# Hybrid layer with a two-level expert stage on one core: smaller expert blocks, longer weight runs, gathers that skip empty slots, another order of products and outputs

## The chip, the cores and the metric

One core of a Trainium2 chip runs the whole layer as one program. The metric is device time in microseconds, the median of several runs. A core has a matrix engine (TensorE, PE in the profile, with PEld for its weight loads), VectorE (DVE), ScalarE (ACT), GpSimd (POOL) and SyncE (SP), which mostly issues transfers, and 16 DMA engines.

## What is computed

A layer over 512 latent tokens (and 256 context tokens) of width 1024. After the mixer (convolution and gated linear attention, one output projection, a layer norm), each token is routed to one of four groups and to two experts in it:

```python
group_prob = softmax(tok @ wgr + bgr);  p_g, g_idx = top_k(group_prob, 1)
sel = expert_logits[group g_idx];       top_w, top_i = top_k(softmax(sel), 2)
for e in range(16):                     # D_MODEL 1024, D_EXPERT 512
    act = silu(tok @ w1[e]) * (tok @ w3[e])
    out = out + combine[:, e:e + 1] * (act @ w2[e])
x = layer_norm(alpha * x + g2 * out)
```

`tok` is the normed mixer output, scaled and shifted by a condition (`modulate`). All weights are f32: 2 MB each for `w1[e]`, `w3[e]` and `w2[e]`, 96 MB for the 16 experts.

## The kernel before

The first half (to about 316 us) is the mixer: projections in f32 split into two parts (`hi` and `lo`, three products for one), the scans, the output projection, the norm. The normed tokens go to DRAM as `tokd` (L940), the residual part to `yd`.

The expert stage works on slots. After routing, the experts are ranked by their token counts; rank j has `CAPS[j]` slots (L45) and the ranks run in the order `ORDER` (L46). Two first jobs (`NE`, `NE + 1`) take up to 128 tokens of experts 0 and 1 before the ranks are known. What is over a capacity is redone by the loop at the end (L1583), which here has no passes.

- A job with 128 or 256 slots is a `BigJob` (L1216) of one or two blocks of 128. Its weights are split by `split` (L377): ScalarE casts a piece to `whi` (L389), VectorE, for some pieces POOL, subtracts to `wlo` (L391). `load` transposes the gathered rows to `Xh`/`Xl` (hi and lo, L1204 to L1206). `hidden` makes per half `c` of the 512 hidden columns the products with `w1` and `w3` (256 columns each, eight steps of contraction, three products a step), then silu and the gate (L1252, L1253) and a transpose. `outputs` makes 24 products of 512 columns, multiplies into `ob` (L1269) and scatters with an add into `yd` (L1182).
- A job with 64 or 32 slots is a `SmallJob` (L1280): `R` = 2 or 4 column groups side by side in one PSUM tile, plain f32 weights without a split, `ob` at L1340. The last job (`obw`, L1336) skips the scatter; its share is added by a product in `finish`.
- Each expert's weights come as six pieces of 1 MB (L978 to L999): `w1` and `w3` cut by columns (`[128, 8, 256]`, runs of 1 KB in DRAM), `w2` by rows (`[128, 2, 1024]`, runs of 4 KB). The pieces go through a ring of twelve buffers (`RING`, L986), issued on SP's queue in job order. 12 of the 96 pieces are issued before 356 us.
- `gather` (L1175) is an indirect DMA from `tokd` on POOL's queue. Empty slots read the 128 zero rows behind the tokens (L890, L896); their indices are T and up (`dumc`, L1025).
- The main loop (L1481) does for job n: issue the weights of job n + 1, `hidden` of n, one-hot tables for later jobs, `load` of n + 1, `prep_next` (slot indices and gather of n + 3), `outputs` of n. The tile framework may reorder instructions within an engine by need and priority; buffers have fixed counts (`whi` and `wlo` four each of half a piece, six PSUM banks for products, two for transposes).
- `finish` (L1513) reads `yd` back, adds the last job, and norms.

Of the kernel before, what the change touches and what calls it, by code (L numbers as in the profile page):

```python
# [62 lines left out]
def layer(ctx: ExitStack, tc: tile.TileContext, a, out, dbg=None):  # L63
# [179 lines left out]
    def ada_fin(pa, parts, bank, prio):  # L243


        s = sb.tile([P, 512], FT, name="adas", tag="as", bufs=2)
        S.copy(s, pa)
        n = len(parts)
        o = bank()[:, :8 * n].rearrange("p (k q i) -> p q k i", i=2, q=n)
        for j in range(4):  # L250
            mm(o[:, :, j, :], s[:, j * P:(j + 1) * P], sel[:, 0:2 * n], prio, start=True, stop=True)
        ts_ = []
        for q, (c0, hf) in enumerate(parts):
            t = sb.tile([P, 4, 2], FT, name="adac", tag="adac", bufs=4)
            V.tensor_tensor(t, o[:, q], vc(VBA + 8 * c0, hf)[:, :, None].to_broadcast([P, 4, 2]), op=OP.add)
            ts_.append(t)
        return ts_

    class Ada:
# [10 lines left out]
        def fin(self):  # L270
            return ada_fin(self.pa, self.parts, pbg, PR_ADA)
# [7 lines left out]
    def ab_half(dst, sh, sc, hf, g0, b0):  # L279

        def bc2(c0):
            return vc(c0, hf)[:, :, None].to_broadcast([P, 4, 2])
# [242 lines left out]
    rb = sb.tile([P, 20], FT, name="rb")  # L525
    V.memset(g4, 0.0)
    with tc.issue_after(wk_lo.ins):
# [6 lines left out]
        G.dma_start(wr[:, :, 4:20], a["router_expert_w"][0].rearrange("(k p) g -> p k g", p=P))  # L534
        G.dma_start(rb[:, 0:4], dview(a["router_group_b"], 0, [[0, P], [1, 4]]))
# [34 lines left out]
    ab2 = const.tile([P, 2, KC, 2], FT)  # L570
# [308 lines left out]
    wsum = sb.tile([P, 2, 20], FT, name="wsum")  # L879
# [10 lines left out]
    tokd = drp.tile([T + P, D], FT, name="tokd")  # L890
# [7 lines left out]
    lg = sb.tile([P, NT, 20], FT, name="lg")  # L898
# [91 lines left out]
    def load_piece(e, ev, n):  # L990
# [4 lines left out]
        shape = [P, 2, 1024] if nm == "expert_w2" else [P, 8, 256]  # L995
# [178 lines left out]

    def gather(idx, R):  # L1175
# [10 lines left out]
    def transpose_to(src, n, dsts):  # L1186

        for j0 in range(0, n, 4):
            pt = pt_()
            m = min(4, n - j0)  # L1190
            transpose4(pt, [src[:, (j0 + j) * P:(j0 + j + 1) * P] for j in range(m)])
            dsts(j0, m, pt)

    def hilo_ev(hi, lo, mod=False):

        def ev(j0, m, pt):
            f = "p k t -> p (k t)"
            for j in range(m if mod else 0):
                A, B = ab2[:, 0, j0 + j, 0:1], ab2[:, 1, j0 + j, 0:1]
# [15 lines left out]

    class BigJob:  # L1216


        def __init__(self, blocks, first=False):
            self.blocks = blocks  # L1220
# [5 lines left out]
        def load(self):  # L1226
            self.X, self.A = [], []
            for _, _, g in self.blocks:
                x = hl_tiles(KC, "X")
                transpose_to(g, KC, hilo_ev(*x, True))  # L1230
                self.X.append(x)

        def hidden(self, wts):
            for b in self.blocks:
                self.A.append(hl_tiles(4, "A"))
            for c in range(2):
                H = []
                for wi in range(2):
                    his, los = split(wts[2 * c + wi], 256, **self.kws(2 * c + wi))
                    for b, (xh, xl) in enumerate(self.X):  # L1240
                        if wi == 0:
                            H.append((pb_(), Bank()))
                        o, grp = H[b]
                        o = o[:, wi * 256:(wi + 1) * 256]
                        for k in range(KC):
                            grp.mm(o, xh[:, k, :], his[k])
                            grp.mm(o, xh[:, k, :], los[k])
                            grp.mm(o, xl[:, k, :], his[k])
                for b, (_, w, _) in enumerate(self.blocks):
                    o = H[b][0]  # L1250
                    s_ = mo.tile([P, 256], FT, name="s", tag="s", bufs=4)
                    S.activation(s_, o[:, :256], AF.Silu)  # L1252
                    V.scalar_tensor_tensor(s_, o[:, 256:], w, s_, op0=OP.mult, op1=OP.mult)  # L1253
                    hi, lo = self.A[b]
                    transpose_to(s_, 2, hilo_ev(hi[:, 2 * c:2 * c + 2], lo[:, 2 * c:2 * c + 2]))

        def outputs(self, wts):
            W = [split(wts[4 + q], 1024, **self.kws(4 + q)) for q in range(2)]
            for (idx, _, _), (ah, al) in zip(self.blocks, self.A):
                os_ = [pb_() for n in range(2)]  # L1260
# [375 lines left out]
```

## Time and profile before

| | |
|---|---|
| median of 3 runs | 704.65 us (703.65 to 704.81) |
| the profiled execution | 701.98 us, of it the span 700.2 us |
| PE busy | 645.3 us (92%) |
| DVE busy | 474.9 us (68%) |
| ACT busy | 318.5 us (45%) |
| POOL busy | 135.2 us (19%) |
| DMA | 176.79 MB, mean 252 GB/s over the span |
| mean granted clock of TensorE | 0.974 |

The span is the time from the first to the last instruction on the core. An engine's busy share is an average over stages; what a stage is worth is read in that stage. A DMA share of about 1 in a stretch means that the 16 DMA engines were busy all through it.

### The profile page before, as it was taken

The numbers are of one execution on the slowest core, as the hardware profiler recorded it, in microseconds if no ns is written. First come the engines' busy times: TensorE is split into PE (matmuls) and PEld (weight loads), VectorE is DVE, ScalarE is ACT, GpSimd is POOL, SyncE is SP. The second block draws the span as 40 slices with busy tenths as digits, with TensorE's granted clock in tenths as the row PEclk, the third lists the DMA queues.
The fourth block names the chain that finished last, engine by engine and source line by source line (L and its number), as shares of the span: only waits on it lengthen the run. The fifth ranks groups of instructions, "written<-read, shape, count | busy, mean of one in ns | idle before, by whom it ended". The sixth has DMA issues, their size and how long they took to land.

```text
span 700.2 us, 11612 instructions
## 1 busy us (share of the span) xinstructions
PE 645.3 (92%) x4378; PEld 505.8 (72%) x4378; DVE 474.9 (68%) x1036; ACT 318.5 (45%) x505; POOL 135.2 (19%) x106
## 2 busy tenths in 40 slices
PE   5899999989999999996798899998999999999973
PEld 4565689777887787784698598594988588996431
DVE  8545741785965877649899875586669887594245
ACT  3338721458432234325276553454557375471100
POOL 2410000000000100025417312032123221122112
PEclk9999999999999999997799999999999999999998
DMA  8997965372112189626469899899999999979943
GB/s 310 370 338 248 313 197 176 121 230 73 59 62 64 57 294 373 204 91 219 165 204 355 314 338 369 263 369 353 359 367 319 324 369 345 348 216 349 318 142 116
DMA packets 114125, 176.79 MB, mean 252 GB/s; under 512 B 3905, under 2 KB 82129, under 8 KB 114066
## 3 DMA queue, kind: packets, MB, share of 16 engines
q1 hardware_dynamic: 107570, 157.31, 65.4%
q0 software_dynamic: 5136, 15.50, 8.9%
q10 hardware_dynamic: 1360, 3.21, 1.2%
q8 instruction: 36, 0.59, 0.3%
q14 instruction: 23, 0.19, 0.1%
HBM read 160.92 MB, written 15.07 MB: 251 GB/s over the span
## 4 chain that ended last, share of the span: by engine, by line
PE 68%; DVE 17%; ACT 6%; DMA 4%; issue 3%; POOL 1%; DVEq 0%; ACTq 0%
PE pb L144 32%; PE mm L144 21%; PE gl L144 3%; PE pt L154 3%; DVE wlo L391 3%; DMA raw<-in_expert_w_dram 3%; ACT whi L389 2%; PE po L144 2%; PE bg L146 2%; PE tp L154 1%; DVE gg L621 1%; PE pt L144 1%; PE py L144 1%; PE pu L144 1%; DVE gg L620 1%
## 5 line engine op out<-in xcount | busy, mean ns | idle before, releaser
L391 DVE TENSOR_TENSOR wlo<-raw,whi 128x1024 fp32r<-128x1024 f32 x65 | 80.3, 1245 | 50.9 <-ACT whi L389 50.4
L144 PE MATMUL pb<-whi,Xh 128*128 128x256 f32 x384 | 110.6, 289 | 3.7 <-ACT Xh L1205 3.7
L144 PE MATMUL pb<-whi,Xl 128*128 128x256 f32 x384 | 110.2, 288 | 1.6 <-DVE Xl L1206 1.6
L144 PE MATMUL pb<-wlo,Xh 128*128 128x256 f32 x384 | 108.9, 285 | 0.0
L389 ACT CAST whi<-raw 128x1024 fp32r<-128x1024 f32 x68 | 70.9, 1049 | 57.6 <-PE mm L144 26.2
L389 ACT CAST whi<-ew 128x1024 fp32r<-128x1024 f32 x68 | 71.3, 1051 | 29.4 <-PE pb L144 28.2
L144 PEld LDWEIGHTS pb<-whi,Xh 128*128 128x128 f32 x384 | 73.3, 191 | 8.0 <-ACT Xh L1205 7.1
L391 DVE TENSOR_TENSOR wlo<-ew,whi 128x1024 fp32r<-128x1024 f32 x56 | 68.8, 1237 | 12.9 <-ACT whi L389 10.9
L144 PEld LDWEIGHTS pb<-whi,Xl 128*128 128x128 f32 x384 | 73.1, 191 | 2.0 <-DVE Xl L1206 2.0
L144 PEld LDWEIGHTS pb<-wlo,Xh 128*128 128x128 f32 x384 | 73.3, 191 | 0.1
L1182 POOL DMA_INDIRECT yd<-ob,idx x18 | 30.6, 1699 | 103.3 <-DVE ob L1340 31.5
L391 POOL TENSOR_TENSOR wlo<-ew,whi 128x1024 fp32r<-128x1024 f32 x12 | 29.9, 2501 | 86.9 <-issue 70.2
L144 PE MATMUL mm<-hhi,whi 128*128 128x512 f32 x112 | 44.3, 403 | 1.6 <-ACT hhi L368 1.6
L144 PE MATMUL mm<-hhi,wlo 128*128 128x512 f32 x112 | 42.8, 392 | 0.0
L144 PE MATMUL mm<-hlo,whi 128*128 128x512 f32 x112 | 42.5, 390 | 0.0
L294 POOL TENSOR_TENSOR ss<-ss,nhalf 128x4 f32<-128x4 f32 x4 | 5.4, 1357 | 188.8 <-DVE ss L293 188.8
L144 PE MATMUL pb<-wlo,Ah 128*128 128x512 f32 x96 | 38.6, 403 | 0.2 <-DVE wlo L391 0.2
L144 PE MATMUL pb<-whi,Ah 128*128 128x512 f32 x96 | 38.8, 404 | 0.0
L144 PE MATMUL pb<-whi,Al 128*128 128x512 f32 x96 | 38.1, 402 | 0.3 <-DVE Al L1206 0.3
L144 PE MATMUL mm<-wlo,hhi 128*128 128x256 f32 x128 | 36.9, 288 | 0.0
L144 PE MATMUL mm<-whi,hhi 128*128 128x256 f32 x128 | 36.7, 287 | 0.0
L144 PE MATMUL mm<-whi,hlo 128*128 128x256 f32 x128 | 36.6, 286 | 0.0
(418 smaller groups left out, 1445.8 us busy)
## 6 DMA issues: line engine op xcount, KB each, us to landing
ew<-in_expert_w_dram SPq DMA_DIRECT2D x64, 1024.0 KB
raw<-in_expert_w_dram SPq DMA_DIRECT2D x32, 1024.0 KB
raw<-in_w_ada_dram SPq DMA_DIRECT2D x22, 1024.0 KB
raw<-in_w_in_dram SPq DMA_DIRECT2D x10, 1024.0 KB
raw<-in_w_out_dram SPq DMA_DIRECT2D x4, 1024.0 KB
xz<-in_x_dram SPq DMA_DIRECT2D x4, 512.0 KB
ada<-in_w_ada_dram SPq DMA_DIRECT2D x2, 1024.0 KB
x<-in_x_dram SPq DMA_DIRECT2D x4, 512.0 KB
```

Of the source, the lines that this page charges most:

```text
L144: return PE.matmul(o, lhsT, rhs, **kw)
L146: return PE.matmul(o, lhsT, rhs, **kw)
L154: PE.transpose(pool_tile[:, j * P:(j + 1) * P], s, ident)
L294: pows.append(G.tensor_tensor(dst, dst, nhalf[:, :dst.shape[1]], op=OP.pow))
L389: S.copy(hi, r[:, k0:k0 + step, :])
L391: lows.append(lo_eng[k0 // step].tensor_tensor(lo, r[:, k0:k0 + step, :], hi.bitcast(FT), op=OP.subtract))
L620: V.tensor_tensor_scan(g[0:DK, :], mask[0:DK, :n], m[0:DK, :], 0.0, op0=OP.mult, op1=OP.add)
L621: V.tensor_tensor_scan(g[DK:P, ::-1], mask[DK:P, :n], m[DK:P, ::-1], 0.0, op0=OP.mult, op1=OP.add)
L1182: G.indirect_dma_start(out=yd.rearrange("t (r w) -> (t r) w", r=R), out_offset=bass.IndirectOffsetOnAxis(ap=idx[:, :1], axis=0), in_=o, in ...
```

## The change

- `CAPS` becomes `[256, 192] + [128] * 5 + [64] * 3 + [32] * 3 + [31] + [0] * 2`, and `ORDER` is new. A job's capacity is cut into blocks of 128, 64 and 32 (`parts_of`); a job of 192 slots is one `Block` of 128 and one `SmallBlock` of 64.
- All pieces are halves by rows, with a partition holding neighbouring rows (`"o (p k) n -> p (o k) n"`): runs of 8 KB for all three weights. The products with `w1` and `w3` now have 512 columns, and a piece holds four of the eight contraction steps for all columns.
- To match, the transposes take every fourth (`rows_of`) or every second (`every`) column of their source, the condition's scale and shift are made a second time in that order (`abx`, from a second set of small products in `ada_fin` and four small loads `pvec`), and the first job's pick products read `x1` in steps of four.
- `gather` has a bounds check, so that empty slots move nothing; the three gather buffers are zeroed once on POOL, and the 128 zero rows of `tokd` and their two stores are gone.
- `hidden` is a generator with a step per piece; `gate` (silu, gate, transposes) follows all products of the job. The first step of the next job is issued ahead of the outputs of this one.

The diff, cut to what the steps below speak of:

```diff
-CAPS = [256] * 3 + [128] * 4 + [64] * 5 + [32, 31] + [0] * 2
-ORDER = [12, 0, 11, 6, 10, 1, 3, 8, 4, 2, 5, 9, 7, 13]
+CAPS = [256, 192] + [128] * 5 + [64] * 3 + [32] * 3 + [31] + [0] * 2
+ORDER = [12, 11, 0, 9, 1, 8, 2, 7, 3, 4, 5, 6, 10, 13]
...
+        for n_, v_ in enumerate((a["b_ada"][0, 3 * D:4 * D], a["b_ada"][0, 4 * D:5 * D], a["ln1_g"][0], a["ln1_b"][0])):
+            G.dma_start(pvec[:, n_], v_.rearrange("(h p c) -> p h c", h=2, c=4))
...
-    sh0, sc0, sh1, sc1 = ada.fin()
+    (sh0, sc0, sh1, sc1), perm = ada.fin(lambda c0, hf: px(c0 - 3, hf))
     ab_half(ab2, sh0, sc0, 0, V1G, V1B)
     ab_half(ab2, sh1, sc1, 1, V1G, V1B)
+    xp = perm()
+    ab_half(abx, xp[0], xp[1], 0, 2, 3, px)
+    ab_half(abx, xp[2], xp[3], 1, 2, 3, px)
...
-        S.dma_start(tokd[T:T + P, h * 512:(h + 1) * 512], zero)
...
-        src = src[:, h * 256:(h + 1) * 256, :] if nm == "expert_w2" else src[:, :, h * 256:(h + 1) * 256]
-        return src.rearrange("o (k p) n -> p (o k) n", p=P)
+        n = src.shape[1] // 2
+        src = src[:, h * n:(h + 1) * n, :]
+        return src.rearrange("o (p k) n -> p (o k) n", p=P)
...
+    gxs = [mo.tile([P, D], FT, name=f"gx{n}") for n in range(3)]
...
     def gather(idx, R):
-        g = mo.tile([P, D // R], FT, name="gx", tag="gx", bufs=3)
+        g = gxs[ngx[0] % 3][:, :D // R]
+        ngx[0] += 1
         ins = G.indirect_dma_start(out=g, out_offset=None, in_=tokd.rearrange("t (r w) -> (t r) w", r=R),
-                             in_offset=bass.IndirectOffsetOnAxis(ap=idx[:, :1], axis=0))
+                             in_offset=bass.IndirectOffsetOnAxis(ap=idx[:, :1], axis=0),
+                             bounds_check=T * R - 1, oob_is_err=False)
...
+    def every(src, c, j):
+
+        return src.rearrange("s (p c) -> s c p", c=c)[:, j]
+
+    def rows_of(g, hf):
+        return [every(g[:, hf * 512:(hf + 1) * 512], 4, c) for c in range(4)]
...
+    class Block:
...
+        def load(self):
+            self.X = hl_tiles(KC, "X")
+            for hf in range(2):
+                pt = pt_()
+                transpose4(pt, rows_of(self.g, hf))
+                hilo_ev(*self.X, True)(4 * hf, 4, pt)
...
+        def products(self, c, wi, his, los):
+
+            xh, xl = self.X
+            for k in range(4):
+                kc = 4 * c + k
+                mm3(self.H[wi], xh[:, kc, :], xl[:, kc, :], his[k], los[k], kc == 0, kc == KC - 1)
...
+    class SmallBlock:
...
+        def load(self):
...
+            if R == 2:
+                transpose4(pt, [every(self.g, 4, c) for c in range(4)])
+                parts = [(slice(0, P), pt.rearrange("p (c r n) -> p c r n", c=4, r=2))]
+            else:
...
+                for u in range(2):
+                    us = slice(u * 64, (u + 1) * 64)
+                    for c in range(4):
+                        mm(pt[us, c * P:(c + 1) * P], every(self.g, 4, c), ident, start=True, stop=True)
...
+    def parts_of(j):
+
+        c, off, parts = cap_of(j), 0, []
+        while off < c:
+            R = next(R for R in (1, 2, 4) if P // R <= c - off or R == 4)
+            parts.append((R, off))
+            off += P // R
+        return parts
...
+    for g in gxs:
+        G.memset(g, 0.0)
     pick(0)
...
+    steps_ = {seq[0]: jobs[seq[0]].hidden(wts[seq[0]])}
     for n_, j in enumerate(seq):
...
-        jobs[j].hidden(wts[j])
+        for _ in steps_[j]:
+            pass
...
         if n_ + 1 < len(seq):
             jobs[seq[n_ + 1]].load()
+        jobs[j].gate()
         prep_next(n_ + 3)
+        if n_ + 1 < len(seq):
+
+            steps_[seq[n_ + 1]] = jobs[seq[n_ + 1]].hidden(wts[seq[n_ + 1]])
+            next(steps_[seq[n_ + 1]])
```

## Rows read from the trace of the kernel before

**Rows 1.** The page, chain that ended last, shares of the span by engine.

```profile
PE 68%; DVE 17%; ACT 6%; DMA 4%; issue 3%; POOL 1%; DVEq 0%; ACTq 0%
```

**Rows 2.** Timeline of DVE (start us, us, line, operation), two result multiplies.

```profile
397.76 0.68 DVE L1269 TENSOR_TENSOR ob<-pb,g2b 128x512 f32<-128x512 f32 x1
...
670.24 1.98 DVE L1336 SCALAR_TENSOR_TENSOR obw<-pb,sa,g2x 31x256 f32<-31x256 f32 x4 [1.61 <-PE pb L144]
```

**Rows 3.** Busy us by stretch: length, PE, PEld, DVE, ACT, POOL, clock, DMA share, GB/s.

```profile
397.80:403.90 6.10, 5.00 (x62) 2.57 (x55) 4.03 (x15) 2.95 (x8) 2.60 (x2) 1.00 0.61 194
403.90:442.60 38.70, 38.70 (x288) 35.09 (x288) 26.39 (x51) 18.51 (x27) 7.73 (x5) 1.00 1.07 351
442.60:454.60 12.00, 11.97 (x80) 5.98 (x77) 3.65 (x11) 4.10 (x10) 1.57 (x1) 1.00 0.82 235
454.60:480.70 26.10, 24.18 (x184) 19.97 (x184) 20.62 (x40) 14.14 (x18) 8.82 (x5) 1.00 1.08 363
480.70:488.60 7.90, 7.87 (x47) 3.37 (x43) 4.10 (x13) 3.44 (x8) 2.54 (x2) 1.00 1.05 381
488.60:528.30 39.70, 39.70 (x295) 37.01 (x295) 27.82 (x52) 21.66 (x33) 8.09 (x5) 1.00 1.07 356
528.30:549.20 20.90, 20.25 (x154) 16.82 (x153) 19.30 (x30) 13.20 (x17) 5.76 (x3) 1.00 1.06 338
549.20:559.40 10.20, 10.17 (x64) 4.79 (x63) 8.39 (x51) 3.72 (x9) 2.88 (x3) 1.00 0.95 286
559.40:583.50 24.10, 21.73 (x149) 18.84 (x149) 22.13 (x34) 17.07 (x24) 5.07 (x3) 1.00 1.07 360
583.50:621.00 37.50, 37.50 (x276) 34.82 (x276) 25.50 (x45) 20.69 (x31) 9.15 (x6) 1.00 0.95 299
621.00:637.00 16.00, 16.00 (x114) 14.12 (x115) 13.36 (x22) 8.69 (x12) 5.25 (x3) 1.00 1.01 313
637.00:649.90 12.90, 12.87 (x95) 6.92 (x95) 2.55 (x6) 1.30 (x4) 1.60 (x2) 1.00 1.06 352
649.90:663.00 13.10, 12.90 (x90) 6.50 (x90) 2.82 (x11) 1.88 (x5) 1.56 (x1) 1.00 1.05 353
663.00:670.20 7.20, 5.92 (x98) 3.00 (x96) 1.20 (x3) 1.88 (x4) 1.55 (x1) 1.00 0.39 61
```

**Rows 4.** PE: a piece of the chain by time, two starts in the timeline, pick products.

```profile
419.69 8.31 PE pb L144 x70
...
366.03 0.39 PE L144 MATMUL pb<-whi,Ah 128*128 128x512 f32 x1
...
368.83 0.40 PE L144 MATMUL pb<-whi,Ah 128*128 128x512 f32 x1
...
339.85 3.84 PE L144 MATMUL pt<-ohf,x 128*128 128x128 f32 x32 [0.26 <-DVE sa L1163]
```

**Rows 5.** Timeline of PE, the outputs of a job of 64 slots.

```profile
659.31 3.65 PE L144 MATMUL pb<-ew,at 128*64 128x512 f32 x14
```

**Rows 6.** The page's row of POOL's DMA queue; SP's issues from 356 us on.

```profile
q0 software_dynamic: 5136, 15.50, 8.9%
...
356.39 10.48 SPq L997 DMA_DIRECT2D ew<-in_expert_w_dram  x6
```

**Rows 7.** Packets in two windows of 4 us, 428 to 432 and 504 to 508.

```profile
DMA packets 1395, 1.40 MB, mean 349 GB/s; under 512 B 30, under 2 KB 1395, under 8 KB 1395
...
DMA packets 481, 1.63 MB, mean 408 GB/s; under 512 B 22, under 2 KB 103, under 8 KB 481
```

**Rows 8.** Timeline of PE, a wait of the first job's products.

```profile
346.92 0.39 PE L144 MATMUL pb<-whi,Xh 128*128 128x256 f32 x1 [1.61 <-ACT Xh L1205]
```

**Rows 9.** Timelines of POOL and DVE while POOL subtracts, and the first gather.

```profile
326.64 7.07 POOL L391 TENSOR_TENSOR wlo<-ew,whi 128x1024 fp32r<-128x1024 f32 x3 [3.41 <-ACT whi L389]
...
341.53 1.10 POOL L1177 DMA_INDIRECT gx<-tokd,idx  x1 [7.82 <-issue]
...
329.05 2.44 DVE L1154 TENSOR_SCALAR ohf<-slot,posr 128x128 f32<-128x128 bf16 x1
```

More of the change, by code (lines that the diff above doesn't have):

```diff
@@ L1324, in outputs @@
+            pt = pt_()
+            transpose4(pt, [every(hs[:, q * 256:(q + 1) * 256], 2, o) for q in range(m // 2) for o in range(2)])
+            v = pt[:, :m * P].rearrange("p (c i g s) -> p i g c s", i=2, g=gw, s=n)
+            for g_ in range(gw):
+                fs = slice(m * g_, m * g_ + m)
+                S.activation(sg[:, fs], v[:, 0, g_], AF.Silu)
+                V.tensor_tensor(self.at[:, fs], v[:, 1, g_], sg[:, fs], op=OP.mult)
         def outputs(self, wts, wide=None):
             R, n = self.R, self.n
[L1326 removed]
@@ L1339, in outputs, with __init__, kws, hidden @@
             ob = mo.tile([P, ow], FT, name="ob", tag="ob", bufs=2)
-            V.scalar_tensor_tensor(ob, po[:, :ow], w, g2x[R], op0=OP.mult, op1=OP.mult)
-            scatter(ob, idx, R)
+            V.scalar_tensor_tensor(ob, po[:, :ow], self.w, g2x[R], op0=OP.mult, op1=OP.mult)
+            scatter(ob, self.idx, R)
+    class BigJob:
+        def __init__(self, blocks, first=False):
+            self.blocks = [Block(*b) for b in blocks if b[-1] == 1]
+            self.small = [SmallBlock(*b) for b in blocks if b[-1] > 1]
+            self.kw, self.pool = dict(prio=0) if first else {}, ()
+        def kws(self, q):
+            return dict(self.kw, lo_eng=(V, G if q in self.pool else V))
+        def load(self):
+            for b in self.blocks + self.small:
+                b.load()
+        def hidden(self, wts):
+            for b in self.blocks + self.small:
+                b.start()
+            for c in range(2):
+                for wi in range(2):
+                    W = split(wts[2 * c + wi], 512, **self.kws(2 * c + wi))
+                    for b in self.blocks:
+                        b.products(c, wi, *W)
+                    if wi:
+                        for b in self.small:
+                            b.products(c, wts)
+                    yield
+        def gate(self):
+            for b in self.blocks + self.small:
+                b.gate()
+        def outputs(self, wts):
+            W = [split(wts[4 + q], 1024, **self.kws(4 + q)) for q in range(2)]
+            for b in self.blocks:
+                b.outputs(W)
+            for b in self.small:
+                b.outputs(wts)
@@ new lines, in layer, with kws, __init__, hidden @@
+    class FirstJob(BigJob):
+        def kws(self, q):
+            if q < 2:
+                return dict(prio=0, after=lsc, lo_eng=(G, G), lo_after=pows[-1])
+            return BigJob.kws(self, q)
+    class SmallJob:
+        def __init__(self, blocks):
+            self.blocks = [SmallBlock(*b) for b in blocks]
+        def load(self):
+            for b in self.blocks:
+                b.load()
+        def hidden(self, wts):
+            for b in self.blocks:
+                b.start()
+            for c in range(2):
+                for b in self.blocks:
+                    b.products(c, wts)
+                yield
+        def gate(self):
+            for b in self.blocks:
+                b.gate()
+        def outputs(self, wts, wide=None):
+            for b in self.blocks:
+                b.outputs(wts, wide)
@@ L1461, in last_hot @@
         jl = seq[-1]
-        R = jobs[jl].R
+        R, = [R for R, _ in parts_of(jl)]
         n, w = P // R, D // R
@@ L1604, in layer @@
             load_piece(-1, fev, q)
-        job = BigJob([(idx, w, gather(idx, 1)[0])])
+        job = BigJob([(idx, w, gather(idx, 1)[0], 1)])
         job.load()
-        job.hidden(wts[-1])
+        for _ in job.hidden(wts[-1]):
+            pass
+        job.gate()
         job.outputs(wts[-1])
```

218 lines of the change are left out of this document (96 added, 122 removed).

## The prediction

> **What bounds the kernel now.** I read the chain of work that ended last first: PE holds 68% of it and DMA 4% [rows 1]. So matrix work sets the end; the question is which part of the span it does so in. I then cut the expert stage at the moments when a job's last result is multiplied out (the `ob` multiplies and at last the `obw` ones; the first and the last stand in [rows 2], of 27 and 4) and asked each stretch for its busy times [rows 3]. The reader should compare PE's and VectorE's time with the stretch. Two-block jobs take 38.7, 39.7 and 37.5 us with PE full: PE alone. One-block jobs take 26.1, 20.9, 24.1 and 16.0; in the third VectorE works 22.1 of 24.1 us and PE 21.7: both are close, and VectorE leads, since the splitting of six weight pieces costs the same for one block as for two. Jobs of 64 slots take 12.0, 7.9, 10.2, 12.9, 13.1, those of 32 slots 6.1 and 7.2. In nearly every stretch the DMA share is 0.95 to 1.08 as well, so the transfers are a second bound close behind: 84 of the 96 weight pieces are issued from 356.4 us on [rows 6].
>
> **The jobs.** Means by kind: two blocks 38.6, one block 21.8, 64 slots 11.2, 32 slots 6.65 us [rows 3]. PE's own need for a block of 128: 96 products of 256 columns at 8.31/70 = 0.1187 us and 24 of 512 columns at (368.83-366.03)/12 = 0.2333 us [rows 4], with 12 transposes at about 0.11 us (32 in 3.6 us for the like-sized products [rows 4]): 11.4 + 5.6 + 1.3 = 18.3 us. For a block of 64: its outputs take 3.65 us [rows 5]; its first products stream twice as many columns, 7.3; eight transposes 0.9: 11.8 us. The new list after the two first jobs is: one job of 256 (38.6), one of 192, a block of 128 and one of 64 (38.6 - 18.3 + 11.8 = 32.1), five of 128 (109.0), three of 64 (33.6), four of 32 (26.6): 239.9 us. The old list takes 272.4 (397.8 to 670.2). Difference -32.5 us. It is on the path because the stretches lie end to end.
>
> **8 KB runs.** A stretch with only 1 KB packets moves 349 GB/s, one with 4 KB packets 408 [rows 7]. After the change all pieces have runs of at least the longer kind; no row has 8 KB, so I take 408. For the 84 pieces of 1.0486 MB: before 58.7 MB/349 + 29.4/408 = 168 + 72 = 240 us, after 88.1/408 = 216. The gathers' and scatters' queue moves 15.5 MB in 8.9% of 700.2 = 62 us of all engines [rows 6]. By the code, 18 gathers of whole blocks (7.3 MB) become at most 1,024 routed rows of 4 KB (4.2 MB), and the scatters go from 7.7 to 6.7 MB: 62 - 4.1/0.249 = 46 us. The transfers alone would then end at 356.4 + 216 + 46 = 618 instead of 659 us. This gives nothing by itself while PE sets the end, but without it the transfers would hold the jobs back (rival 3). Its result is also a floor: with the 41 us that follow the last landing now, the span could not fall below about 659, the median not below 664, unless 8 KB runs beat 4 KB ones.
>
> **Wider products.** 48 of 512 columns instead of 96 of 256 is 11.2 instead of 11.4 us per block, ten blocks: -2 to 0, taken -1, as one-block jobs lean on VectorE.
>
> **Halves of X.** Weights are now cut along the contraction, so the first piece needs only the first half of the block's columns. The first job's products stall twice for X, 1.61 and 1.64 us (the first stands in [rows 8]): -3.2 to 0, taken -2.
>
> **Order of gate and outputs.** Before, half of the silu chain ran beside the second half of the products. Now the whole chain comes after them, and the next job's first products (12 x 0.2333 = 2.8 us per block) are put in front of the outputs to cover it. I cost this at nothing. If the cover fails, the price is what PE now idles in a stretch where it waits on such chains, 24.1 - 21.7 = 2.4 us [rows 3], times nine big jobs, 21 us; if it covers more than it must, up to the 3.5 us per one-block job of rival 1.
>
> **Blocks of 32.** Their load uses 8 f32 products (16 instructions, 0.112 us [rows 4]) instead of two transposes: 0 (under a wait, and two column groups side by side) to +1.6 us each, four jobs: 0 to +6.3, taken +3.2.
>
> **Zeroing the gather buffers.** Three POOL memsets of 128x1024 stand before the first gather. The nearest rows are POOL's 128x1024 subtractions, 7.07/3 = 2.36 us, and beside those a VectorE operation took 2.44 us [rows 9]: a memset could hold VectorE too. POOL is free between them and the gather, 7.8 us [rows 9]. 0 to +7.1, taken +1.5. Queued behind them on POOL is that gather; its block is needed only after the first job's products.
>
> **Before the experts.** Four small POOL loads (16-byte runs) ahead of the router biases, eight tiny products and some ten small VectorE operations for the permuted modulation, minus two zero stores on ACT's queue: POOL is long before its next need there, and PE's part is a few tenths. 0 to +2, taken +0.3.
>
> **Sum.** -32.5 - 1 - 2 + 3.2 + 1.5 + 0.3 = -30.5 us. Against the profiled execution's 701.98 us (span 700.2) that is 671.5; the median of the runs, 704.65, lies 2.7 above that execution, so **674.1 us**.
>
> **Rivals.** (1) *PE sets the pace of one-block jobs too*, because splits run ahead during small jobs and the new order keeps PE fed. For: one such job took 16.0 us after a two-block job. Against: four now follow one another, and VectorE needs as long as PE. Five jobs at 18.3 instead of 21.8: -17.5, 656.6; with the transfer floor of about 664 in mind I put it at 661.
> (2) *VectorE sets it*, and gates, loads and memsets cost their upper ends: five at 24.1 (+11.5), +3.1, +5.6: 694.
> (3) *The runs bring nothing*: pieces stay at 349 GB/s. Then 252 + 46 = 298 us of transfers from 356.4, end 654 instead of 659, and the last landing decides: -5, 700. For it: the share is 1.1 there already; against: the 4 KB rows. [...]
> (4) *Slower: strided reads on PE.* The contraction is now grouped so that a transpose reads every fourth number of a gathered row. No row of before has PE read in such steps. 64 instructions of the first pick, 72 transposes of nine gathered blocks, 16 of four 64-slot blocks and 64 for the 32-slot ones make 216. At 0.112 us now, doubling them costs 24 us (698, still faster); the sign turns at 30.5/216 = 0.141 us more each, 2.3 times the present pace; at four times it is +73, 747. The place is the load in front of each job, where PE has nothing else ready but the previous outputs. [...]
> (5) *Blocks overflow.* Capacities fall from 1663 to 1407 slots; an expert over its rank's would be redone in the loop at the end with the final stage, over 50 us. The inputs as the reference draws them give counts of 186, 134, 109, 100, 94, 71, 70, 61, 56, 53, 5, 5, 3, 1 by rank: all fit. Under 0.01.
>
> **Chances.** Forecast (664 to 686) 0.58; rival 1, 0.20; rival 2 and a mild form of 4 (686 to 700) 0.12; rival 3, 0.03; rival 4 in full 0.05; something that eats all, 0.02. The range 656 to 694 leaves out part of the last four, about 0.17. A measurement of this kernel tells about 0.2% from no change; by that, faster 0.93, same 0.02, slower 0.05.
>
> **What would show it.** Cut by job again: one-block jobs at 21 to 23 us with VectorE about as busy as PE confirm the main term; 18 us is rival 1. Windows with weight loads alone should show 400 GB/s or more, and gaps in the DMA share where there were none. The transposes of gathered rows should still run at about 0.11 us; 0.25 or more is rival 4. PE idle between a job's last products and its outputs would show the gate uncovered. The forecast is wrong if one-block jobs keep above 25 us, or if the last landing still decides.

## The result, and the profile after

The changed kernel takes 727.14 us (median; 725.26 to 728.40) against 704.70 us before: 1.032 times as long, 95% interval 1.0292 to 1.0348. Forecast were 674.1 us, in a range of 656 to 694. The profiled execution took 725.26 us, its span 723.5 against 700.2.

Below, all runs were timed beside runs of the kernel before on the same chip, whose median went from 702.4 to 704.7 us, so they are compared by their ratio to it; 0.01 is 7 us.

The chain of work that ended last, kernel after, shares of the span by engine (the line to [rows 1]):

```profile
PE 65%; DVE 17%; ACT 7%; DMA 5%; issue 5%; POOL 1%; ACTq 0%; SPq 0%; DVEq 0%
```

Busy times cut by job, kernel after (to be read beside [rows 3]; the first stretch is the second whole job, the others are the ranks 12, 11, 0, 9, 1, 8, 2, 7, 3, 4, 5, 6, 10, 13). Columns: stretch, length, busy us of PE, weight loads, VectorE, ACT, POOL, then granted clock, DMA share, GB/s:

```profile
392.50:416.00 23.50, 19.55 (x108) 12.75 (x107) 15.64 (x30) 6.43 (x9) 9.19 (x5) 0.85 0.96 342
416.00:428.30 12.30, 10.93 (x154) 6.37 (x153) 9.24 (x22) 4.48 (x7) 4.22 (x2) 1.00 0.88 294
428.30:443.20 14.90, 12.87 (x88) 9.18 (x86) 10.94 (x31) 8.44 (x17) 2.64 (x2) 0.89 1.02 412
443.20:483.30 40.10, 37.15 (x163) 25.88 (x163) 21.38 (x39) 13.09 (x18) 7.63 (x5) 1.00 0.84 311
483.30:495.80 12.50, 10.46 (x55) 5.50 (x51) 8.94 (x21) 5.86 (x10) 3.15 (x2) 1.00 0.77 222
495.80:528.50 32.70, 32.16 (x142) 17.48 (x144) 17.53 (x28) 12.63 (x16) 5.34 (x4) 1.00 0.63 222
528.50:542.70 14.20, 12.16 (x61) 5.73 (x57) 7.82 (x18) 5.86 (x10) 3.42 (x2) 1.00 1.00 357
542.70:572.10 29.40, 24.88 (x100) 15.13 (x102) 21.44 (x54) 11.69 (x14) 7.11 (x5) 0.88 1.02 404
572.10:585.70 13.60, 11.57 (x51) 6.07 (x48) 9.61 (x24) 5.85 (x10) 2.65 (x2) 0.87 1.02 377
585.70:612.80 27.10, 23.47 (x102) 18.66 (x103) 20.19 (x28) 17.55 (x24) 5.04 (x3) 0.94 0.83 322
612.80:636.80 24.00, 20.35 (x90) 16.12 (x89) 20.02 (x30) 16.40 (x23) 5.79 (x3) 0.93 0.88 331
636.80:660.70 23.90, 20.26 (x89) 16.05 (x88) 19.93 (x30) 16.31 (x23) 6.74 (x4) 0.93 0.70 240
660.70:680.60 19.90, 17.78 (x103) 12.17 (x105) 11.09 (x17) 6.17 (x9) 4.65 (x2) 0.91 0.87 326
680.60:690.80 10.20, 8.77 (x122) 5.49 (x118) 3.52 (x12) 2.40 (x5) 1.56 (x1) 1.00 0.33 54
690.80:696.50 5.70, 4.13 (x66) 2.03 (x58) 0.95 (x4) 0.82 (x3) 1.56 (x1) 1.00 0.26 33
```

Read it in three parts. *The list* (416.0 to 696.5) takes 280.5 us against 272.4 before; forecast were 239.9. *Up to the end of the second whole job* it takes 416.0 against 397.8, 18.2 more. *The tail* takes 27.0 against 30.0. 18.2 + 8.1 - 3.0 = 23.3, the difference of the spans. Against the forecast the list loses 40.6: four jobs of 32 slots 16.5 (43.1 for 26.6), five one-block jobs 15.3 (124.3 for 109), three of 64 slots 6.7, the two large ones 2.1. The transfers, a close second bound before, have gaps now in most stretches of the list (shares of 0.63 to 0.88 in eight of the fourteen, 1.00 to 1.02 in four). And in the one-block job of 24.0 us neither PE (20.35) nor VectorE (20.02) fills the stretch, and PE's granted clock, 1.00 in all stretches of [rows 3], is 0.93. PE waits; for what, the timelines show. Between two one-block jobs, kernel after, PE, then ACT, then VectorE (start, us; in brackets the idle time before, and what ended it):

```profile
594.10 1.12 PE L155 MATMUL pt<-ident,gx 128*128 128x128 f32 x8
598.84 0.80 PE L145 MATMUL pb<-whi,Xh 128*128 128x512 f32 x1 [3.63 <-ACT Xh L1230]
599.57 0.70 PE L155 MATMUL pt<-ident,s 128*128 128x128 f32 x2
...
594.30 1.05 ACT L397 CAST whi<-ew 128x1024 fp32r<-128x1024 f32 x1 [0.27 <-PE pb L145]
595.25 0.77 ACT L1229 ACTIVATE pt<-pt,abx 128x128 f32<-128x128 f32 x2
597.18 0.78 ACT L1229 ACTIVATE pt<-pt,abx 128x128 f32<-128x128 f32 x2 [1.16 <-DVE pt L1227]
598.20 1.07 ACT L1230 CAST Xh<-pt 128x512 fp32r<-128x512 f32 x2 [0.25 <-DVE pt L1227]
...
594.06 1.22 DVE L399 TENSOR_TENSOR wlo<-ew,whi 128x1024 fp32r<-128x1024 f32 x1 [0.26 <-DMA ew<-in_expert_w_dram]
...
596.73 0.73 DVE L1227 TENSOR_SCALAR pt<-pt,abx 128x128 f32<-128x128 f32 x2
597.37 0.48 DVE L1270 SCALAR_TENSOR_TENSOR s<-pb,sa,s 128x256 f32<-128x256 f32 x1
```

The next job's rows are transposed at 594.1. Their modulation alternates between ACT and VectorE, behind a splitting on either, and PE's next instruction, the next job's first product, stands until `Xh` is there. The gate's transposes (`pt<-ident,s`, from 599.57) and the outputs (from 604.04) come only behind it; the second half of the gate's product `s` was itself made at 597.37, between parts of X, so the two chains share VectorE. PE's longest waits from 400 to 660 us by cause: first the kernel after (31.9 us in all), then the kernel before (5.5 in all; total us, times, longest):

```profile
PE pb L145 <- ACT Xh L1230: 19.1, 7, 3.7
PE pb L145 <- DVE xt L1317: 5.6, 3, 2.8
PE pt L155 <- DVE xt L1316: 4.8, 3, 3.4
```

```profile
PE pt L154 <- ACT hs L1313: 1.8, 1, 1.8
PE pt L154 <- DVE Xl L1206: 1.5, 3, 0.9
PE pb L144 <- ACT Xh L1205: 0.7, 3, 0.2
```

At the start of the experts, kernel after: POOL, two small VectorE operations, the picks, and a wait of PE before the second job:

```profile
325.92 2.73 POOL L1485 MEMSET gx<- 128x1024 f32 x3 [2.48 <-DVE pg L1122]
328.61 9.36 POOL L399 TENSOR_TENSOR wlo<-ew,whi 128x1024 fp32r<-128x1024 f32 x4
...
328.96 2.12 DVE L1127 TENSOR_TENSOR wc<-dn,pg 128x4 f32<-128x4 f32 x1
331.11 2.27 DVE L1128 TENSOR_TENSOR wc<-wc,dw 128x4 f32<-128x4 f32 x1
...
338.40 7.70 PE L145 MATMUL pt<-ohf,x 128*128 128x128 f32 x32 [8.41 <-issue]
346.44 7.74 PE L145 MATMUL pt<-ohf,x 128*128 128x128 f32 x32 [0.26 <-DVE sa L1183]
...
377.89 0.80 PE L145 MATMUL pb<-whi,Xh 128*128 128x512 f32 x1 [6.21 <-ACT Xh L1230]
```

After the three memsets, four POOL subtractions follow one another, and four small VectorE operations beside them take over 2 us each (two shown). That is not new: the kernel before has four subtractions there too (three of them in [rows 9]) and four VectorE operations of over 2 us, and PE waits for the one-hot tables in the first half of the picks:

```profile
331.55 0.80 PE L144 MATMUL pt<-ohf,x 128*128 128x128 f32 x2 [4.03 <-DVE ohf L1154]
333.99 5.52 PE L144 MATMUL pt<-ohf,x 128*128 128x128 f32 x26 [1.65 <-DVE ohf L1154]
```

Counted from the first expert load (246.71 before, 252.33 after), these 26 start at 87.3 us, and all 32 of the kernel after at 86.1. What is new is the pace of the second half, 0.24 us each instead of 0.12 [rows 4]. Of the 18.2 us ahead of the list, 5.6 have passed at the first expert load and 10.5 at the end of the picks (354.2 against 343.7); the other 7.7 fall in the first two jobs, where the wait of 6.21 us stands.

### The profile page after: what moved, and what is told of

Its sections match the earlier page's. It is cut to its first block, busy times and chain, and to the rows that moved or that the text cites. A ratio compares the mean times of both kernels' runs of the same rounds, so it can differ in the third digit from the quotient of the medians.

```text
span 723.5 us, 10168 instructions
## 1 busy us (share of the span) xinstructions
PE 635.5 (88%) x3678; PEld 461.0 (64%) x3678; DVE 473.8 (65%) x1024; ACT 309.5 (43%) x479; POOL 137.9 (19%) x111
## 4 chain that ended last, share of the span: by engine, by line
PE 65%; DVE 17%; ACT 7%; DMA 5%; issue 5%; POOL 1%; ACTq 0%; SPq 0%; DVEq 0%
PE pb L145 27%; PE mm L145 21%; DVE wlo L399 5%; PE gl L145 3%; PE pt L145 3%; PE pt L155 3%; PE bg L147 2%; PE po L145 2%; ACT whi L397 2%; PE tp L155 1%; DMA ew<-in_expert_w_dram 1%; DVE xt L1317 1%; DMA raw<-in_w_ada_dram 1%; DVE gg L641 1%; DMA l1g<-in_ln_g_dram 1%
## 5 line engine op out<-in xcount | busy, mean ns | idle before, releaser
L399 DVE TENSOR_TENSOR wlo<-ew,whi 128x1024 fp32r<-128x1024 f32 x72 | 91.8, 1292 | 39.5 <-ACT whi L397 37.3
L145 PE MATMUL pb<-whi,Xh 128*128 128x512 f32 x160 | 69.1, 433 | 25.3 <-ACT Xh L1230 25.3
L399 DVE TENSOR_TENSOR wlo<-raw,whi 128x1024 fp32r<-128x1024 f32 x49 | 61.6, 1273 | 40.5 <-ACT whi L397 40.3
L145 PE MATMUL pb<-wlo,Xh 128*128 128x512 f32 x160 | 66.6, 416 | 0.4 <-POOL wlo L399 0.4
L145 PE MATMUL pb<-whi,Xl 128*128 128x512 f32 x160 | 66.7, 417 | 0.0
L145 PEld LDWEIGHTS pb<-whi,Xh 128*128 128x128 f32 x160 | 31.7, 198 | 36.8 <-ACT Xh L1230 27.0
L1202 POOL DMA_INDIRECT gx<-tokd,idx x17 | 22.6, 1332 | 110.7 <-DVE idx L1191 41.7
L145 PE MATMUL pb<-raw,xt 128*32 128x256 f32 (+1 forms) x224 | 35.4, 488 | 7.0 <-DVE xt L1317 7.0
L145 PEld LDWEIGHTS pb<-wlo,Xh 128*128 128x128 f32 x160 | 32.2, 201 | 7.0 <-POOL wlo L399 0.9
L145 PEld LDWEIGHTS pb<-whi,Xl 128*128 128x128 f32 x160 | 31.8, 199 | 7.0
L399 POOL TENSOR_TENSOR wlo<-ew,whi 128x1024 fp32r<-128x1024 f32 x12 | 28.8, 2416 | 33.8 <-issue 27.1
```

Of the source, the lines that this page charges most:

```text
L145: return PE.matmul(o, lhsT, rhs, **kw)
L399: lows.append(lo_eng[k0 // step].tensor_tensor(lo, r[:, k0:k0 + step, :], hi.bitcast(FT), op=OP.subtract))
```

## The experiments

Theory A: the wait for X in front of ready outputs is the loss. Theory B: strided reads on PE. Theory C: transfers, when the products shrink.

**Run b1: the blocks alone, on the kernel before.**

```diff
-CAPS = [256] * 3 + [128] * 4 + [64] * 5 + [32, 31] + [0] * 2
-ORDER = [12, 0, 11, 6, 10, 1, 3, 8, 4, 2, 5, 9, 7, 13]
+CAPS = [256] * 2 + [128] * 5 + [64] * 3 + [32] * 3 + [31] + [0] * 2
+ORDER = [12, 11, 0, 9, 1, 8, 2, 7, 3, 4, 5, 6, 10, 13]
```

> The kernel before with the new capacities and the new order of experts alone (the rank of 192 slots takes 256, as this code has no mixed job). The forecast's main term: the list becomes 2 x 38.6 + 5 x 21.8 + 3 x 11.2 + 4 x 6.65 = 246.4 instead of 272.4 us, so 704.7 - 26 = 679. If PE sets the pace of one-block jobs, 665. Rival: two small jobs and a two-block job at the front bring weights late, and the prices by kind do not carry over to the new order: 690 or more.

Measured: 692.46 us, ratio 0.985 [0.9818, 0.9882]. A gain of some 10 us, not 26. Busy times of the ranks 11 and 4, and the wait of the first:

```profile
401.30:416.60 15.30, 9.15 (x105) 4.73 (x98) 7.29 (x12) 6.62 (x12) 2.58 (x2) 0.83 1.09 359
579.20:604.10 24.90, 22.43 (x142) 19.99 (x142) 18.90 (x28) 15.92 (x22) 4.98 (x3) 0.91 1.07 352
```

```profile
ACT whi L389 <- DMA ew<-in_expert_w_dram: 7.4, 1, 7.4
```

The blocks gain, but my prices by kind don't carry over: the two small jobs at the front take 7.4 and 15.3 us instead of 6.65 each (ACT stands 7.4 us for a weight piece, the DMA share is 1.09), the five one-block jobs 117.6 us together instead of 109.

**Run u1: the first products behind the outputs again.**

```diff
-            steps_[seq[n_ + 1]] = jobs[seq[n_ + 1]].hidden(wts[seq[n_ + 1]])
-            next(steps_[seq[n_ + 1]])
...
             jobs[j].outputs(wts[j])
+            steps_[seq[n_ + 1]] = jobs[seq[n_ + 1]].hidden(wts[seq[n_ + 1]])
```

> The kernel after, with the next job's first products put back behind the outputs of the job that runs (the gate stays whole, after all products). Theory A: in the kernel after PE, which works in order, waits for the next job's X in front of outputs that are ready; it waited 25.3 us for Xh and 9.1 us for xt in the expert stage. Then most of these waits go, some are replaced by the wait for the gate's A, and the time falls from 727 to 700-715. Theory B: the strided reads on PE and the slower prelude are the loss; the order matters little, the gates now stand uncovered: 727-745.

Measured: 725.75 us, 1.0318 [1.0282, 1.0354]. No change, so the order alone is not the loss, and theory A in this form falls. With load and gate both after the products, the outputs now wait behind the same two chains: the gate's transposes stand until X has been read out of the transposes' PSUM tiles (PE from 400 to 660 us):

```profile
PE pt L155 <- DVE Xl L1231: 22.4, 7, 4.7
```

**Run b2: strided reads alone, on the kernel before.** Columns and weights don't match in it; the work is the same.

```diff
-            transpose4(pt, [src[:, (j0 + j) * P:(j0 + j + 1) * P] for j in range(m)])
+            v = src[:, j0 * P:(j0 + m) * P].rearrange("s (p c) -> s c p", c=m)
+            transpose4(pt, [v[:, j] for j in range(m)])
```

> The kernel before with the picks and all transposes of the expert stage reading every fourth (every second) column instead of neighbours; it leaves the grouping of the weights as it was, so the columns meet the wrong weights, and the work is the same. Theory B: 64 pick products at +0.13 us and some 150 transposes at +0.07 us: 704.7 to 713-724. Rival: such reads cost only where PE is the bound, so only the picks: 709-713. No cost of strides at all: 704-706.

Measured: 706.1 us, 1.0053 [1.0035, 1.0071]: 3.7 us more than the kernel before beside it, 708.4 on the base of the expectations. That is just below theory B's rival, strides that cost in the picks only, and far from theory B. In its trace the picks end 101.7 us after the first expert load, 97.0 in the kernel before; the list takes 275.2 for 272.4.

**Run u5: the next job's X beside the products.**

```diff
-        for _ in steps_[j]:
-            pass
+        for k_, _ in enumerate(steps_[j]):
+            if early and nxt is not None and k_ == (n_ == 0):
+                nxt.load()
+                nxt = None
...
-            jobs[seq[n_ + 1]].load()
+        if nxt is not None:
+            nxt.load()
```

> The kernel after with the next job's X made in the middle of the running job's products (where no more than two X are alive; after a job with two blocks as it was). Theory D: PE stands still because the chains of X and of the gate both run on ACT and VectorE only after the last product; with X beside the products the 2.0-3.65 us waits for Xh and xt before ten jobs go and the one-block jobs take 20.5-21.5 instead of 23.9 us: 727 to 700-710. Rival E: VectorE and ACT are the bound (20.0 of 23.9 us busy) and the wait moves elsewhere: 718-728.

Measured: 711.07 us, 1.0097 [1.0064, 1.0130]: 2.2% less than after. Busy times of a one-block job (rank 5; rank 4 takes 21.35 too):

```profile
621.18:642.53 21.35, 19.18 (x90) 15.02 (x89) 19.45 (x30) 15.86 (x23) 6.74 (x4) 1.00 1.01 388
```

Theory D of its expectation holds: 21.35 instead of 23.9 us, as it said, and the clock is back at 1.00. The time, at 711, ends a little above its bracket. In the trace the list takes 264.4 us instead of 280.5, and from the end of the picks to that of the second whole job pass 53.8 instead of 61.8 (before 54.1); the tail, 33.1, is 6.1 longer than in the kernel after.

**Run u2b: contiguous reads** (w1 and w3 in 2 KB runs, w2 in 4 KB, no second set of modulation columns; the 32-slot blocks load with two transposes again).

```diff
-        return src.rearrange("o (p k) n -> p (o k) n", p=P)
+        return src.rearrange("o (k p) n -> p (o k) n", p=P)
...
-        return src.rearrange("s (p c) -> s c p", c=c)[:, j]
+        return src[:, j * P:(j + 1) * P]
```

> The kernel after with contiguous reads on PE: weight rows grouped so that 128 neighbouring columns belong to one chunk (w1 and w3 in 2 KB runs, w2 in 4 KB), picks and transposes read neighbours; the permuted modulation and its four small loads are gone. The kernel before with strided reads lost only 3.7 us, so from the reads alone 4-8 us come back and from the missing small loads up to 5: 727 to 714-720. If the long runs matter in the jobs (theory C: transfers become the bound as soon as the products shrink), less, 720-728. If strides are the main loss: 700-708.

Measured: 709.36 us, 1.0081 [1.0051, 1.0111]: 2.4% less than after, more than b2 lets expect and below the 714 to 720 forecast for it. The trace says where: the first expert load comes 5.5 us earlier, from there to the end of the picks it is 5.3 less, the first two jobs take 3.4 less and the tail 1.0 less. The list, 279.9, is the same as after.

**Run c1: u5 and u2b together.**

> Contiguous reads (as in the run u2b) and the next job's X made beside the products (as in the run u5) together. If the two are independent: 727 - 17.5 - 16 = 693.5. If the shorter runs of w1 and w3 (2 KB) now hold the transfers at 370 GB/s or less and these set the pace: 697-705.

Measured: 694.16 us, 0.9882 [0.9835, 0.9929]. The two gains add (4.4%), and this version beats both kernels. Busy times of the ranks 11, 7 and 4:

```profile
411.30:430.40 19.10, 14.49 (x105) 9.44 (x98) 15.27 (x34) 12.14 (x21) 2.65 (x2) 0.91 1.05 378
549.00:566.70 17.70, 13.41 (x58) 6.49 (x57) 13.37 (x27) 9.21 (x14) 3.63 (x2) 0.90 1.04 371
590.40:611.60 21.20, 19.01 (x90) 14.62 (x89) 19.38 (x29) 15.77 (x23) 5.65 (x3) 1.00 1.04 374
```

**Run c3: c1 without the reordering** (u1's edit on c1; X stays beside the products).

> The run c1 (contiguous reads, X beside the products) with the next job's first products behind the outputs again. Theory: with X ready the products ahead cover the gate, whose chain of silu, product, transposes and two copies lasts 3.5-4.5 us, of which they hide 2.8-5.6; ten jobs with large blocks lose 2-3 us each without it: 694 to 712-724. Rival: the scheduler finds other work for PE, or transfers set the pace: 692-700.

Measured: 700.4 us, 0.9975 [0.9951, 0.9999], 0.9% above c1. With X ready the reordering does what it is for and is worth some 6.5 us, less than the theory's 18 and near its rival.

**Run c8: c1 with 8 KB runs.**

> The run c1 with the weights of all jobs loaded in 8 KB runs (the columns then meet other weight rows; the work is the same). In c1 weights moved at 370-384 GB/s with a DMA share of 1.04-1.06 in the one-block jobs, where VectorE was busy 19.4 of 21.2 us as well. Theory C (transfers bind there): at 400 GB/s the stretch with full share, some 150 us, shrinks by 5-6%: 694 to 684-689. Rival (VectorE or PE binds, 19 to 19.4 of 21.2): 692-696.

Measured: 691.98 us, 0.9835 [0.9813, 0.9858], 0.5% below c1 with intervals that overlap. Theory C's 684 to 689 is not reached: by the ratios the long runs then bring some 3 us, by their intervals 7 at most.

**Which part of u2b counts?** Run u3 loads the second set's vectors as rows, u7 reads its products' columns plainly, u9 leaves the whole set out (its blocks use the unfitting first set); u8 makes the picks plain, u10 the transposes of gathered rows (in u7, u8 and u10 columns and weights don't match).

```diff
-            G.dma_start(pvec[:, n_], v_.rearrange("(h p c) -> p h c", h=2, c=4))
+            G.dma_start(prow[2 * n_:2 * n_ + 2], v_.rearrange("(h f) -> h f", h=2))
...
-            return ts_, lambda: columns(lambda j: s.rearrange("r (p c) -> r c p", c=4)[:, j], perm)
+            return ts_, lambda: columns(lambda j: s[:, j * P:(j + 1) * P], perm)
...
-    xp = perm()
+    V.tensor_copy(abx, ab2)
...
-                grp.mm(pt[:, k * P:(k + 1) * P], rows_of(x1[i], hf)[k], ohf[:, i, :])
+                grp.mm(pt[:, k * P:(k + 1) * P], x1[i][:, ks], ohf[:, i, :])
...
-                transpose4(pt, rows_of(self.g, hf))
+                transpose4(pt, [self.g[:, hf * 512 + c * P:hf * 512 + (c + 1) * P] for c in range(4)])
```

> The kernel after with the four vectors of the permuted modulation loaded as 8 rows of 2 KB in place of 1,024 runs of 16 bytes, and brought into columns by four tiny products on PE. Theory: the 16-byte runs hold up the w_ada and w_in loads, and the first expert load moves from 252.3 back to 247-248, time -4 to -5: 722-723. Rival: the prelude is late for another cause (run-to-run of the first loads): 726-728.

> The kernel after with the eight small products of the permuted modulation reading neighbours instead of every fourth column (so the modulation's order doesn't fit; the work is the same). In the trace of the kernel after they are followed by 5.7 us in which products of 256 columns come every 0.213 us instead of 0.119 us, and the next w_ada load is issued 4.3 us late. Theory F: the strided reads pull PE's clock down there; with neighbours the pace stays 0.119, the first expert load comes at 247-249 us, and the time is 722-724. Rival: eight more products and their small VectorE work are the cost, reads of any kind: no change, 726-728.

> The kernel after with the 64 products that pick the first job's rows reading neighbours (the first job's columns then meet other weight rows; the work is the same). Theory: 0.24 us each come back to 0.11-0.12 in the second half at least, first `ob` 5-8 us earlier, 727 to 719-722. Rival: the low parts and the clock, not the strides, set the picks' pace: under 2 us.

> The kernel after without the second, permuted set of modulation columns (its four loads, eight products and VectorE work; the expert blocks use the first set, whose order doesn't fit). Theory: the prelude's 5 us come from this set as a whole: first expert load at 247-251 us, time 727 to 721-723. Rival: the prelude varies from run to run for other reasons: 726-728.

> The kernel after with the transposes of all gathered rows reading neighbours (their columns then meet other weight rows; the work is the same, the eight products per 32-slot block stay). Theory: strided transposes in the jobs cost about 7 us, as between the runs u5 and c6 (287.0 and 280.1 us from the first `ob` to `obw`): 727 to 719-722. Rival: while X stands in front of the outputs, PE waits for ACT and VectorE anyway and its transposes are hidden in front of them: 725-728.

Measured: u3 1.0356 [1.0305, 1.0407], u7 1.0333 [1.0301, 1.0364], u8 1.0319 [1.0290, 1.0348], u9 1.0299 [1.0240, 1.0357], u10 1.0330 [1.0288, 1.0372]. None differs from 1.032 by more than its interval. In u8 the 64 picks do get faster (9.1 us of busy time instead of 15.4 in the same window), and the time doesn't follow. In its trace the gain lasts to the end of the second whole job, 155.9 us after the first expert load (163.7 in the kernel after), but that load is 3.7 us later, the list 3.0 and the tail 2.7 longer; whether that is chance or a next limit is open. In the traces the second set has a mark: the first expert load is issued at 246.7 to 251.4 us in all nine kernels without it (mean 248.9) and at 251.8 to 256.7 in all eleven with it (mean 254.1). SP in the kernel after:

```profile
252.33 0.34 SPq L1017 DMA_DIRECT2D raw<-in_expert_w_dram  x1
```

Part of this spread is older than the set's products. From SP's issue of a `w_in` load at 84 to 90 us on, the first expert load follows after 162.5 us in the kernel before, 162.6 in u9 and 167.0 in the kernel after. In between, the kernel after has the set's eight products and behind them a stretch at a granted clock of 0.50, where the kernel before has 1.00 (busy times as above, kernel after, then before):

```profile
89.44 1.92 PE L147 MATMUL bg<-sel,adas 128*128 128x8 f32 x8
...
91.20:97.00 5.80, 5.80 (x28) 5.80 (x29) 5.45 (x21) 0.37 (x1) 0.00 (x0) 0.50 0.20 63
```

```profile
91.20:97.00 5.80, 5.80 (x47) 3.86 (x46) 4.35 (x13) 1.55 (x4) 0.00 (x0) 1.00 0.46 150
```

1.9 and half of 5.8 make 4.8 us, about what is lost there. With other loads the lag stays (u3, 167.3), with plain reads of the products it is a little less (u7, 165.9), and c4, further down, which reads them from a copy in order, has 163.4. So the set costs the prelude some 4.5 us through PE; u9's timing is too wide to show them in the whole time.

**Runs c4 and c6: keep 8 KB runs, avoid strides otherwise.** c4 is u5 with only the first job contiguous; c6 is u5 with rows put in order by ACT before they are stored for the gathers.

```diff
-        S.dma_start(tokd[i * P:(i + 1) * P, :], x1[i])
+            S.copy(xp_.rearrange("t (c p) -> t c p", c=4), x1[i][:, cs].rearrange("t (p c) -> t c p", c=4))
+            S.dma_start(tokd[i * P:(i + 1) * P, cs], xp_)
```

> The run u5, and the first job alone on contiguous reads (its w1 and w3 in 2 KB runs, its picks reading neighbours, the permuted modulation read from a copy that ACT puts in order); all other jobs keep 8 KB runs and strided transposes. If prelude and picks are what strides cost, and long runs help the jobs: 711 - 5 - 7 = 699, and below the run c1 if transfers bind there. Rival: strided transposes cost as much in the jobs: 703-708.

> The run u5 (X beside the products, 8 KB runs) with the rows put in permuted order by ACT before they are stored for the gathers, so that all transposes of gathered rows read neighbours; picks and the gate keep their strides, the 32-slot blocks load with two transposes. If the strided transposes are what u2b removed, and long runs cost nothing: 711 - 10 to 17 = 694-701; if long runs also help against c1: 686-693. If the strides in the jobs don't matter: 708-712.

Measured: c4 704.84 us, 0.9998 [0.9967, 1.0028]; c6 706.2 us, 1.0011 [0.9972, 1.0051]. Each gains some 1% on u5, neither reaches c1. In c6's trace the time from the first `ob` to `obw` falls from 287.0 to 280.1 us, near c1's 279.7, but its start is later than u5's (the first `ob` 140.8 us after the first expert load, not 133.0): the copies on ACT seem to take back what the plain transposes give.

**Runs u4, c7, c9: the zeroing.** u4 takes the skipping back altogether; c7 (on c6) and c9 (on c1) let ACT zero the buffers.

```diff
-        G.memset(g, 0.0)
+        S.activation(g, x1[0], AF.Copy, scale=0.0)
```

> The kernel after without the skipping of empty slots: gathers read the zero rows behind the tokens as before, the three memsets on POOL are gone, the zero rows are stored again. Theory: the memsets and what they push together on POOL and VectorE cost the start of the experts 3-6 us; without them the picks start 3-6 us earlier and the time is 721-724. Rival: the first products wait for other things (weights' low parts, strided picks): 726-728, or more by the larger gathers.

> The run c6 with the three gather buffers zeroed by ACT instead of POOL. Theory: POOL's three memsets push its low-part subtractions, 2.3 us each, into the stretch in which VectorE makes the one-hot rows, and VectorE stands beside them; without them the picks start 3-4 us earlier: c6 less 3-4. Rival: transfers of the first weights set the pace of the first four jobs, so what the picks gain is lost again: within 1 us of c6.

> The run c1 with the gather buffers zeroed by ACT instead of POOL. Theory: POOL's memsets push its low-part subtractions into the one-hot stretch and the picks start 3-4 us late: 694 to 689-691. Rival: the early jobs are paced by their weights, the gain is lost there: 693-695.

Measured: u4 730.06 us, 1.0382 [1.0326, 1.0439]; c7 699.97 us, 0.9945 [0.9929, 0.9962]; c9 693.24 us, 0.9856 [0.9795, 0.9917]. POOL in c9:

```profile
329.69 4.67 POOL L399 TENSOR_TENSOR wlo<-ew,whi 128x1024 fp32r<-128x1024 f32 x2 [8.77 <-ACT whi L397]
338.12 1.22 POOL L1191 DMA_INDIRECT gx<-tokd,idx  x1 [3.75 <-issue]
```

Only two subtractions are left in the router's stretch. The picks start 78.2 us after the first expert load instead of 86.1 in c1. At the end of the picks 4.1 of these 8 us are left, and c9's time can't be told from c1's. c7's picks start 3.6 us and end 6.0 us earlier than c6's, and its time is 0.7% less (intervals just apart). u4, which has no memsets, is no faster, and its picks end 101.5 us after the first expert load, 101.9 in the kernel after: the skipping as a whole doesn't hurt.

## Why the prediction was wrong

**Order of gate and outputs, costed at nothing: the step that failed most.** I asked whether the gate is covered, and not what the covering products themselves need. Before, the chain that makes X (eight transposes, eight modulations, two copies, two subtractions) ran under the outputs, and PE waited 0.7 us for `Xh` in 260 us. Put in front, the products wait for the whole chain, 594.1 to 598.8, and the gate's transposes and the outputs stand behind them: PE waits 29.5 us in all for this chain (`Xh` and `xt`) in these 260 us, and its granted clock is lower behind the waits (0.52 from 598.84 to 602.40 us, 1.00 from there to 612.8). u5 shows it: 2.2%, with 16.1 us less in the list and 8.0 in the first two jobs. u1 shows that it is the place of the X chain after the products, not the order alone; c3, that the order is a gain of 0.9% once X is ready. My price for a failed cover, 21 us, was near by luck: it was for the wrong chain.

**The jobs: -32.5 in the sum, +8.1 in the trace.** The pace of one-block jobs was right once PE doesn't wait (21.35 in u5, 21.2 in c1, forecast 21.8; ranks 2, 3, 4, 5, 6 take 101.7 us in c1, forecast 109). The small jobs were mis-sized. I took 6.65 us from two rows [rows 3], one behind the whole jobs with its weights landed, one the last, for which nothing more is loaded. A job brings six pieces whatever its slots, and by my own 408 GB/s these 6.3 MB take 15.4 us. Behind one another, ranks 12 and 11 take 22.7 in b1 and 25.8 in c1 for 13.3; in b1 a wait for weights is seen, in c1 and after the load of the next job's two blocks falls into the same stretch. Jobs of 64 slots take 41.9 for 33.6 in c1, of it 17.7 in rank 7, at a DMA share of 1.04. At the start of rank 7's stretch ACT has waited for a piece of the next job's weights, which it then splits ahead of the next job's X, and PE waits for that X:

```profile
548.72 2.00 ACT L397 CAST whi<-ew 128x1024 fp32r<-128x1024 f32 x2 [7.76 <-DMA ew<-in_expert_w_dram]
...
557.03 0.55 PE L145 MATMUL pb<-whi,Xh 128*128 128x512 f32 x1 [4.29 <-ACT Xh L1219]
```

c1's list, cut at the ends of the multiplies as in the rows above, takes 256.4 us (257.8 by the cut of the other kernels), 16.5 over 239.9: these two kinds make 20.3, the large jobs 3.5, and the one-block jobs give 7.3 back.

**8 KB runs** reach 404 and 412 GB/s in two stretches of the kernel after, as taken from the 4 KB row [rows 7]; that they bring nothing by themselves was right (c8: under 1%). Rival 3 is out.

**Strided reads, rival 4.** The weight loads show the price. Kernel after, then before (mean ns after the comma):

```profile
L155 PEld LDWEIGHTS pt<-ident,gx 128*128 128x128 f32 x80 | 11.6, 209 | 5.0 <-issue 3.8 <-DVE Xl L1231 0.7
L155 PEld LDWEIGHTS pt<-ident,s 128*128 128x128 f32 x36 | 6.0, 207 | 13.2 <-issue 9.5 <-DVE xt L1316 1.8 <-DVE Xl L1231 1.3
```

```profile
L154 PEld LDWEIGHTS pt<-ident,gx 128*128 128x128 f32 x112 | 12.6, 140 | 6.8 <-DVE pt L1202 2.4 <-DVE Xl L1206 2.1 <-DVE Al L1206 1.8
```

140 becomes 209 ns (210 and 205 in b2, where only the reads differ), half of the 0.141 us at which I put the turn; on the old kernel that is 3.7 us (b2). So the cost is there and does not turn the sign by itself. Steps of two (`s`, 207 ns; 140 in the kernel before) cost the same as steps of four; my count of 216 had left them out. What contiguous reads give in the changed kernel (2.4%) is more than b2, and more than its parts alone (u3, u7 to u10, each within its interval). By u2b's trace it lies in the prelude, the picks and the first two jobs: while X stands in front, the edit takes only 0.6 us off the list. With X out of the way it takes off 6.6 (u5 264.4, c1 257.8). Why the parts ahead of the list don't show in the time when they come alone is open.

**Zeroing, +1.5.** u4, without memsets, is no faster, so no cost shows. The three memsets take 2.73 us on POOL; beside the subtractions behind them four small VectorE operations take 2.07 to 2.31 us, as one of 2.44 us did in the row that I cited [rows 9], but in the kernel before there were four of 2.06 to 2.44 us as well. What c9 and c7 gain at the picks, 4 to 6 us, comes with two subtractions instead of four beside the router's work; on the time it is 0 (c9) to 4.6 us (c7).

**Before the experts, +0.3:** about 4.5 us, mis-sized by the clock. I counted the eight products as a few tenths; they take 1.9 us, and the products behind them run at a granted clock of 0.50 for 5.8 us. How far the strided reads bring that about is open (u7 against c4).

**Halves of X, -2:** the first job's two waits for `Xh` are gone, as forecast, but the second job's wait of 6.21 us took their place. **Blocks of 32, +3.2,** and the wider products were not measured alone; in c6, which loads these blocks with two plain transposes, their four jobs take 3.4 us less than in u5.

The forecast said that one-block jobs above 25 us would make it wrong; two of five are (29.4 and 27.1), and the gap that I had told to look for, between last products and outputs, is where PE waits. The cause that u5 shows is X's chain, not the gate's; what the gate, now whole and after all products, costs by itself no run shows. Of the forecast's 30.5 us c1 reaches about a quarter.

## What to carry to other kernels

When work is moved ahead of other work on an engine that stands at the first instruction that has to wait, as PE did here (3.63 us at the product of 598.84), price the whole chain that feeds the moved work, and where that chain ran before; a cover that has to wait is no cover. A price per kind of job holds only in the order in which it was read: check each against the bytes that it brings and against what its neighbours load in its stretch. And a change of several parts is best undone in pairs too, since single parts may hide behind each other's waits, as contiguous reads did in the list behind X.

## What the runs showed of the hardware that I had not expected

- A weight load of 128x128 f32 in the transposes (`pt<-ident`) takes 207 ns for steps of two and 209 for steps of four numbers in the kernel after, 205 and 210 in b2, and 140 without steps in the kernel before.
- VectorE operations on 128x4 to 128x16 numbers took 2.07 to 2.31 us beside POOL's subtractions of 128x1024, which take 2.34 each: there a small operation lasted about as long as the large one beside it. The first of them (`wc<-dn,pg`, 2.12) took 0.16 in the kernel before, between two subtractions.
- One-block jobs with a wait of 3.63 to 3.65 us for X ran at a granted clock of 0.93 to 0.94 in the mean (kernel after, ranks 3 to 5), ranks 4 and 5 without the long wait (u5) at 1.00. Around the wait that ends at 598.84 it was 1.00 from 589.0 to 594.1, 0.52 from 598.84 to 602.40 and 1.00 from there to 612.8. The first product behind such a wait takes 0.80 us in the trace (row of 598.84), twice the 0.39 to 0.40 of [rows 4].
- Eight products of 8 columns, 1.92 us of PE, were followed by 5.8 us at a granted clock of 0.50 (kernel after, from 91.2 us).
